# RWKV "wkv" recurrence on one core: rows of w and u on another queue, other tiles for the first loads, half of the last numerators in other PSUM banks, and a new hand-placed order at both ends

## The chip, the cores and the metric

The kernel runs on one core of one Trainium2 chip. The core has TensorE (PE; its weight loads are listed as PEld), VectorE (DVE), ScalarE (ACT), GpSimd (POOL) and SyncE (SP, used here only to issue DMAs). The metric is device time in microseconds (us) of one execution, as the median of several runs. All inputs lie in HBM and the output goes back there.

## The reference

For each of 16 batches and 256 channels a scalar recurrence runs over 2048 steps. It is cut here to one step:

```python
ww = u + kk                       # output of step t
qq = np.maximum(pp, ww)
e1 = np.exp(pp - qq); e2 = np.exp(ww - qq)
output[b, t, :] = (e1 * aa + e2 * vv) / (e1 * bb + e2 + 1e-08)
ww = pp - w + kk                  # state for step t + 1
qq = np.maximum(ww, kk)
e1 = np.exp(ww - qq); e2 = np.exp(kk - qq)
aa = e1 * aa + e2 * vv
bb = e1 * bb + e2
pp = qq
```

`k`, `v` and the output are (16, 2048, 256) in float32, 33.5 MB each; `w` and `u` have 256 values.

## The kernel before, in words

The 2048 steps are cut into 16 chunks `c` of 128 steps (two halves of 64), and the 16 batches into 4 groups of 4. One tile `n` (0 to 63) is one chunk of one group: `c, p = divmod(n, 4)`. It holds 128 steps on the partitions and 4 x 256 channels, 512 KB of `k` and as much of `v`. Inside a half, the recurrence is done with cumulative logarithms, triangular matrices and a division; between halves a small state is carried.

Each tile passes these steps, named as in the scheduler:

- `LK n`, `LV n`: the DMAs of k and v (lines 100 to 111). The first few go on SP (`n < BYSP`), the others on POOL's queue.
- `RK n`: k is rounded into a tile that PE may read (line 189, DVE or POOL, as `how(n)` says; "D" DVE, "P" POOL, "C" no rounding, the DMA writes such a tile itself).
- `R q n`, `L q n` (q = 0, 1): on PE, the rows of w and u (line 196), and then the cumulative sums of k (line 202), are added up in one of two PSUM tiles X, which are handed round in turn. (Each is a pair of PSUM banks; "a bank" means one X below.)
- `X q n`: ACT takes the exponential of X into a ring EZR of 11 tiles (line 205).
- `CV n`, `TV n`: v is cast to bf16 (line 209, DVE for n < 10, then POOL), and DVE multiplies it with both exponentials (line 214).
- `S n`: 8 matmuls of PE add up each half into TOT (line 240).
- `DEN n`, `NUM n`: 12 matmuls each on PE, the denominator into an X tile and the numerator into the one tile `num` (line 317), 10 tiles behind the exponentials.
- `LN n`, `INV n`: ACT forms ln of the denominator from X (line 325) and exp of its negative (line 329), in one of two tiles `rd`.
- `MUL n`: DVE multiplies numerator and inverse into an output tile `ot` (line 337).
- `ST n`: SP stores it in one DMA of 256 KB and two of 128 KB (lines 350 and 343). From tile 52 on the last 128 KB go on POOL's queue as `SQ n`.

Once in a chunk, when `S` of its four tiles is done, the state moves on: `CS` (DVE copies TOT), `TU` (PE turns it), `SL` (ACT), `FR`, `OF` (DVE), `SW` (ACT), `CH`, `SS`, `KP` (DVE), `TK` (PE turns it back), `BK` (DVE copies it for `DEN` and `NUM` of the next chunk) and `SN`.

Before some steps of PE the kernel issues matmuls of zeros into TURN, "zeros" (line 144): `Z` says how many before which step, `Z0` the same for tile and chunk 0. 38 stand at the very start.

The order of all this is written out by a small scheduler (lines 358 to 438). Each step has a place on an axis of tiles; the scheduler always emits the lowest place whose predecessors are done and whose buffer is free. The places come from the table `P`, by `n % 4` in the middle, with another slope for the last 10 tiles (`TAIL`). Every engine then executes its steps in the order of emission and waits by semaphores. Buffers are counted in `free`: `K` rounded k (4), `KP` raw k (5), `V` raw v (4), `VB` cast v (2), `N` the numerator's tile (1), `RD` (2), `OT` output tiles (8).

The rows of w and u go on ACT's DMA queue into one `rd` tile (line 117), and `wu` casts and combines them on DVE (lines 170 and 171).

Of the kernel before, what the change touches and what calls it, by code (L numbers as in the profile page):

```python
# [7 lines left out]
F32 = mybir.dt.float32  # L8
# [3 lines left out]
ACT = mybir.ActivationFunctionType  # L12
# [3 lines left out]
def kernel(  # L16
# [9 lines left out]
    K = tc.keep_in_program_order  # L26
# [10 lines left out]
    SOON = 0  # L37
    UNTIL = 16
# [10 lines left out]
    BYQ = "PSSP"  # L49
    BYF = 93  # L50
    FILL = 1
    P = {"LK": -4.45, "LV": -3.2, "RK": [-2.85, -1.165, -3.305, -1.485], "L": [-12.055, -8.285],
         "X": [-1.875, -0.74], "CV": [0.915, -1.225, -0.805, -4.96], "TV": [-1.505, 1.745, 1.29, 1.32],
         "S": [2.74, -4.135, 2.105, -1.96], "wu": -0.98, "mats": -9.17,
         "STATE": [[-7.49, 2.76, -5.41, 2.15, -0.24, 3.49, -6.31, -2.72, -4.26, 6.5, 5.66, 3.32], [2.48, -1.26, -10.66, 3.23, -8.74, -6.75, 4.23, 2.99, 4.44, -5.61, -28.95, -22.63], [-0.45, 0.53, 6.83, 8.8, 7.73, 14.16, 12.07, 7.09, 13.89, 18.61, 6.68, 11.48]],
         "R": [-0.795, -7.965],
         "OUT": {"DEN": [-0.47, -0.155, -0.55, -0.495], "LN": [-11.935, -9.86, -0.84, -6.17], "INV": [-13.87, -8.32, -4.99, -5.82], "NUM": [-0.105, 0.155, 0.11, -5.15], "MUL": [1.115, 0.345, 0.895, 1.035], "ST": [-5.05, 7.26, 1.245, 7.765], "SQ": [-3.365, 6.69, -2.4, 8.84]},
         "TAIL": {"DEN": -4.36, "LN": -16.54, "INV": 3.8, "NUM": -0.31, "MUL": 4.39, "ST": 14.35, "step": 2.989, "SQ": 26.08},
         "Z0": {"L": 1, "S": 3, "DEN": 0, "NUM": 6, "TK": 47, "TU": 17, "R": 12},
         "Z": {"DEN": 0, "L": 1, "NUM": 0, "TK": 4, "S": 0, "TU": 1, "R": 0}}  # L60

# [53 lines left out]

    def row_wu(x, g):
        K(SC.dma_start(out=WUf[g::32, :], in_=bass.AP(tensor=x.tensor, offset=x.offset, ap=[[0, 4], list(x.ap[0])])))
# [24 lines left out]
    def zeros(m, first=False):  # L142
        for j in range(m):
            K(PE.matmul(TURN[:, 0:192], Z[:, 0:128], Z, start=first, stop=True, skip_group_check=True))  # L144

    zeros(38, True)

# [175 lines left out]
    def log_den(n, a):  # L323
        rd = rpool.tile([128, 2, D], F32, tag="rd", name="rd")
        K(SC.activation(rd, X[a], ACT.Ln, scale=RS))  # L325
        RD[n] = rd

    def inverse(n):
        K(SC.activation(RD[n], RD[n], ACT.Exp, scale=-1.0))  # L329

    def num(n):
        NUM[n] = psn.tile([128, 2, D], F32, tag="num", name="num")
        apply(NUM[n], n, ("SN", "IdN"), 0)

    def mult(n):
        o = opool.tile([128, 4, Dm], F32, tag="ot", name="ot")
        K(DVE.tensor_mul(o.rearrange("p (i n) d -> p i (n d)", i=2), NUM.pop(n), RD.pop(n)))  # L337
        OT[n] = o
# [21 lines left out]
    def step(name, place, fn, args=(), after=(), take=None, give=(), mode=0):  # L360
        ops[name] = dict(place=place, fn=fn, args=args, after=list(after), take=take, give=give, mode=mode)

    for n in range(NP):
        c, j = divmod(n, 4)
        early = n < BYSP
        put = lambda key: n + P[key][j]
# [4 lines left out]
        kb = "V" if early else "KP" if how(n) != "C" else "K"  # L371
        if n:
            step(("LK", n), n + P["LK"], load_k, (n,), [("LK", n - 1)], kb)
        else:
            free["V"] -= 1
        step(("LV", n), n + P["LV"], load_v, (n,), [("LV", n - 1)] + ([("LK", n)] if n else []), "V")
        if how(n) != "C":
            step(("RK", n), put("RK"), round_k, (n,), [("LK", n), ("RK", n - 1)], "K", [kb])
        for q in range(2):
# [3 lines left out]
            step(("X", q, n), n + P["X"][q], exps, (n, q), [("L", q, n), ("NUM", n - RING), ("S", n - RING)], None, ["X"])  # L383
        step(("CV", n), put("CV"), cast_v, (n,), [("LV", n), ("CV", n - 1)], "VB", ["V"])
        step(("TV", n), put("TV"), times_v, (n,), [("X", 1, n), ("CV", n), ("TV", n - 1)], None, ["VB"])
# [13 lines left out]
        step(("INV", n), place("INV"), inverse, (n,), [("LN", n)])  # L399
        step(("NUM", n), place("NUM"), num, (n,), [("BK", c), ("TV", n), ("NUM", n - 1), "mats"], "N", mode=3)  # L400
        step(("MUL", n), place("MUL"), mult, (n,), [("NUM", n), ("INV", n), ("MUL", n - 1)], "OT", ["N", "RD"])
        step(("ST", n), place("ST"), store, (n,), [("MUL", n), ("ST", n - 1)], None, [] if shared(n) else ["OT"])
# [8 lines left out]
    while todo:  # L411
        for name in todo:
            o = ops[name]
            if all(x not in ops or "done" in ops[x] for x in o["after"]) and (xs if o["take"] == "X" else free.get(o["take"], 1)):
                break
        else:
            raise AssertionError(todo[:9])
        todo.remove(name)
        args = list(o["args"])
        if o["take"] == "X":  # L420
            held[name] = xs.pop(0)
            args.append(held[name])
# [4 lines left out]
        if o["give"] == ["X"]:  # L427
            x = held[("DEN", name[1]) if name[0] == "LN" else ("R",) + name[1:]]
            xs.append(x)
            args.append(x)  # L430
        else:
            for x in o["give"]:
                free[x] += 1
# [35 lines left out]
```

## Time and profile before

| what | value |
|---|---|
| median of 3 runs | 293.96 us (293.93 to 294.11) |
| profiled execution | 294.72 us, span of its instructions 293.0 us |
| granted TensorE clock, mean | 0.987 |
| DMA | 101.20 MB, mean 345 GB/s |
| ACT, line 205, 128 exponentials | 126.8 us busy, 1014 ns each |
| ACT, lines 329 and 325, 64 each | 67.8 and 65.7 us, 1059 and 1026 ns |
| DVE, lines 337 and 214, 64 each | 78.1 and 77.7 us, 1220 and 1217 ns |
| PE, zeros, line 144, 331 | 56.4 us busy |
| first exponential on ACT starts | 10.13 us |
| last product on DVE starts | 285.67 us |

The busy time of PE counts matmuls that overlap, so it is a share of time with a matmul under way and no measure of how much of the array is used. A line of a timeline gives the start, the time to the end of the last of its instructions, engine, line, operation, output and inputs, form and number; in brackets the idle time of the engine just before it and what ended that.

The program has three stages. In the fill, to about 48 us, loads, exponentials and the first state build up the distance of 10 tiles. In the middle, a tile takes 4.04 us. In the drain, from about 258 us, there are only outputs.

### The profile page before, as it was taken

The page shows a single profiled execution, that of the slowest core. Times are in us where ns is not written, and L with a number is a line of the kernel's source. Part 1 is how long each engine was busy: PE and PEld are TensorE (multiplying, and loading weights), DVE is VectorE, ACT ScalarE, POOL GpSimd, SP SyncE. Part 2 cuts the span into 40 slices and gives each one's busy share as a digit, 9 for nine tenths or more (in the row PEclk, how much of TensorE's full clock was granted, in tenths as well). Part 3 has the DMA queues.
Part 4 walks back from the last instruction along what each step waited for, and adds up shares of the span by engine and source line. Part 5 has one row for each costly group of instructions (what it writes and reads, how often), then busy time and mean ns, then how long its engine had stood idle before and what let it go on. Part 6 is the DMA issues. An engine that isn't in the chain of part 4 may idle for free.

```text
span 293.0 us, 8081 instructions
## 1 busy us (share of the span) xinstructions
PE 273.6 (93%) x3275; PEld 140.2 (48%) x3275; DVE 247.2 (84%) x422; ACT 258.7 (88%) x289; POOL 175.6 (60%) x218
## 2 busy tenths in 40 slices
PE   7899998999999999999999999999999999997750
PEld 7445743454545444444545444554544454543420
DVE  6574859989898989989898989899899989697751
ACT  1486498999999999999999999999999999997970
POOL 6167339575768677575767686775757574431230
PEclk9999999999999999999999999999999999999995
DMA  7999999999999999999999999999999999956884
GB/s 221 349 240 353 346 350 297 380 365 394 380 397 380 380 391 385 391 378 397 383 391 372 392 388 391 395 387 392 391 386 372 394 359 389 313 156 189 221 245 136
DMA packets 58549, 101.20 MB, mean 345 GB/s; under 512 B 5128, under 2 KB 43536, under 8 KB 58512
## 3 DMA queue, kind: packets, MB, share of 16 engines
q0 software_dynamic: 21216, 65.54, 64.8%
q1 hardware_dynamic: 37280, 35.14, 35.7%
q8 instruction: 25, 0.41, 0.6%
q14 instruction: 12, 0.10, 0.1%
q10 hardware_dynamic: 16, 0.01, 0.0%
HBM read 67.12 MB, written 33.55 MB: 344 GB/s over the span
## 4 chain that ended last, share of the span: by engine, by line
PE 70%; DMA 10%; DVE 5%; issue 5%; ACT 4%; POOL 3%; POOLq 0%; SPq 0%; ACTq 0%; DVEq 0%
PE X L202 17%; PE X L317 15%; PE num L317 12%; PE X L196 10%; PE TURN L144 9%; PE TOT L240 6%; DMA kf<-in_k_dram 4%; DMA vr<-in_v_dram 3%; DVE ot L337 2%; DMA WUf<-in_u_dram 2%; PE TOT L253 2%; ACT EZR L205 1%; DVE EZR L214 1%; PE TURN L297 1%; ACT rd L329 1%
## 5 line engine op out<-in xcount | busy, mean ns | idle before, releaser
L205 ACT ACTIVATE EZR<-X 128x1024 bf16<-128x1024 f32 x128 | 126.8, 1014 | 14.9 <-PE X L202 14.9
L209 POOL CAST vb<-vr 128x1024 bf16<-128x1024 f32 x54 | 56.4, 1044 | 71.3 <-DVE EZR L214 67.9
L337 DVE TENSOR_TENSOR ot<-num,rd 128x1024 f32<-128x1024 f32 x64 | 78.1, 1220 | 8.6 <-PE num L317 5.1
L214 DVE TENSOR_TENSOR EZR<-EZR,vb 128x2048 bf16<-128x2048 bf16 x64 | 77.7, 1217 | 0.3
L329 ACT ACTIVATE rd<-rd 128x1024 f32<-128x1024 f32 x64 | 67.8, 1059 | 2.0
L325 ACT ACTIVATE rd<-X 128x1024 f32<-128x1024 f32 x64 | 65.7, 1026 | 3.5 <-PE X L317 1.2
L144 PE MATMUL TURN<-Z 128*128 128x192 bf16 x331 | 56.4, 259 | 1.6 <-DVE Z L128 1.6
L110 POOL DMA_DIRECT2D vr<-in_v_dram x61 | 46.0, 755 | 13.9 <-DVE kr L189 7.1
L196 PE MATMUL X<-WU,CO 64*64 64x512 bf16 x512 | 51.9, 390 | 1.6 <-DVE WU L171 1.3
L144 PEld LDWEIGHTS <-Z 128*128 128x128 bf16 x331 | 29.6, 101 | 48.9 <-issue 47.1
L202 PE MATMUL X<-kr,NLE 128*128 128x512 f32 x128 | 45.6, 438 | 0.0
L202 PE MATMUL X<-kr,NLZ 128*128 128x512 f32 x128 | 45.5, 437 | 0.0
L103 POOL DMA_DIRECT2D kf<-in_k_dram x53 | 40.2, 758 | 0.0
L189 DVE CAST kr<-kf 128x1024 fp32r<-128x1024 f32 x39 | 32.0, 849 | 5.9 <-DMA kf<-in_k_dram 5.8
L317 PE MATMUL num<-EZR,SN 64*64 64x512 bf16 x256 | 25.9, 387 | 6.5 <-DVE ot L337 6.5
L196 PEld LDWEIGHTS <-CO 64*64 64x64 bf16 x512 | 15.7, 105 | 31.8 <-issue 26.9
L317 PE MATMUL X<-EZR,S 64*64 64x512 bf16 x256 | 26.2, 394 | 0.7 <-ACT EZR L205 0.3
L317 PE MATMUL X<-cb,Id 64*64 64x512 bf16 x256 | 25.8, 376 | 0.0
L317 PE MATMUL X<-EZR,Id 64*64 64x512 bf16 x256 | 25.8, 376 | 0.0
L317 PE MATMUL num<-cb,IdN 64*64 64x512 bf16 x256 | 25.8, 378 | 0.0
L317 PE MATMUL num<-EZR,IdN 64*64 64x512 bf16 x256 | 25.6, 376 | 0.0
L240 PE MATMUL TOT<-EZR,OH 128*32 128x256 bf16 x512 | 23.7, 277 | 1.2 <-DVE EZR L214 1.2
(63 smaller groups left out, 259.3 us busy)
## 6 DMA issues: line engine op xcount, KB each, us to landing
vr<-in_v_dram POOLq DMA_DIRECT2D x61, 512.0 KB, 7.8
kf<-in_k_dram POOLq DMA_DIRECT2D x53, 512.0 KB, 8.7
out_dram<-ot SPq DMA_DIRECT2D x64, 256.0 KB, 9.7
out_dram<-ot SPq DMA_DIRECT2D x116, 128.0 KB, 10.0
kr<-in_k_dram POOLq DMA_DIRECT2D x8, 512.0 KB, 8.5
vr<-in_k_dram SPq DMA_DIRECT2D x3, 512.0 KB, 5.2
vr<-in_v_dram SPq DMA_DIRECT2D x3, 512.0 KB, 6.1
out_dram<-ot POOLq DMA_DIRECT2D x12, 128.0 KB, 3.0
```

What stands on the lines that cost most here:

```text
L110: K((SP if n < BYSP else POOL).dma_start(out=vr, in_=rows_of(v, n)))
L144: K(PE.matmul(TURN[:, 0:192], Z[:, 0:128], Z, start=first, stop=True, skip_group_check=True))
L196: K(PE.matmul(X[a][o:o + HS, i, :].rearrange("p (n d) -> p n d", n=2), CO[r:r + HS, q, :], WU[r:r + HS, :].unsqueeze(1).broadcast_to([HS, ...
L202: K(PE.matmul(X[a][:, i, :], (NLE, NLZ)[q], km[:, i, :], start=False, stop=True, skip_group_check=True))
L205: K(SC.activation(ez(n)[:, q, 1], X[a], ACT.Exp))
L209: K((DVE if n < EARLY else POOL).tensor_copy(vb, VR.pop(n)))
L214: K(DVE.tensor_mul(ez(n)[:, :, 0], ez(n)[:, :, 1], vb.unsqueeze(1).broadcast_to([128, 2, 2, D])))
L240: K(PE.matmul(t[32 * j:32 * j + 32, 0:256], OH[:, s:s + 32], ez(n)[:, 0, 1 - q, i, 256 * x:256 * x + 256], start=p == 0 and x == 0, stop=p ...
L317: K(PE.matmul(out_tile[o:o + HS, i, :], left, right, start=s == 0, stop=s == 2, tile_position=(r, o), skip_group_check=True))
L325: K(SC.activation(rd, X[a], ACT.Ln, scale=RS))
L329: K(SC.activation(RD[n], RD[n], ACT.Exp, scale=-1.0))
L337: K(DVE.tensor_mul(o.rearrange("p (i n) d -> p i (n d)", i=2), NUM.pop(n), RD.pop(n)))
```

## The change

The diff has these parts.

1. The row of u and then that of w are loaded on SP's queue, right behind k 0, instead of w and u on ACT's. `wu` is placed ahead of the rounding of k 0.
2. `BYSP` 4 for 3: k 3 and v 3 also go on SP. The raw tiles of k 0 to k 3 and v 0 to v 2 are taken from the pool of output tiles, which now has 10 tiles (8 before). `NK` is 3 (4), `NV` 3 (4).
3. Which engine rounds the first 12 k is written out: `FIRST = "DPDCCCCCPCCP"`, with "D" for n < 4.
4. From tile 56 on, the numerators of odd tiles go to an X tile (`by_x`), which comes free when its product is done; the scheduler can therefore free two kinds of buffer in one step.
5. For the last tile, the inverse and the product are done in two halves.
6. The first zeros are 26 (38), those in the tables differ by a few; `TK` of the middle has 3 (4).
7. The table `P` has new values throughout, and a new table `AT` gives single steps a place of their own, for tiles 0 to 19 and 50 to 63; it overrides `P`.

```diff
-    BYSP = 3
+    BYSP = 4
-    NK, NKP, NV, NVB, NRD, NOT = 4, 5, 4, 2, 2, 8
+    NK, NKP, NV, NVB, NRD, NOT = 3, 5, 3, 2, 2, 10
-    CF = 11
+    FIRST = "DPDCCCCCPCCP"
+    VOT = 3
+    XT = 8
...
-         "S": [2.74, -4.135, 2.105, -1.96], "wu": -0.98, "mats": -9.17,
+         "S": [2.43, -4.915, 1.825, -2.27], "wu": -5.05, "mats": -9.3,
...
-         "Z0": {"L": 1, "S": 3, "DEN": 0, "NUM": 6, "TK": 47, "TU": 17, "R": 12},
-         "Z": {"DEN": 0, "L": 1, "NUM": 0, "TK": 4, "S": 0, "TU": 1, "R": 0}}
+         "Z0": {"L": 1, "S": 5, "DEN": 5, "NUM": 5, "TK": 50, "TU": 16, "R": 11},
+         "Z": {"DEN": 0, "L": 1, "NUM": 0, "TK": 3, "S": 0, "TU": 1, "R": 0}}
+    AT = {"LV 0": -4.6, "RK 0": -2.3975, "R 0 0": -1.8739, "L 0 0": -11.62, "X 0 0": -2.16, "R 1 0": -7.3021,
...
     def how(n):
-        return "D" if n < BYSP else "C" if n < CF else PLAN[n % len(PLAN)]
+        return "D" if n < BYSP else FIRST[n] if n < len(FIRST) else PLAN[n % len(PLAN)]
...
-            KR[n] = raw(vpool, "vr") if n < BYSP else raw(kppool, "kf")
+            KR[n] = raw(opool, "ot") if n < BYSP else raw(kppool, "kf")
...
-        vr = raw(vpool, "vr")
+        vr = raw(opool, "ot") if n < VOT else raw(vpool, "vr")
...
     load_k(0)
-    row_wu(w, 0)
-    row_wu(u, 1)
+    row_wu(SP, u, 1)
+    row_wu(SP, w, 0)
...
-    zeros(38, True)
+    zeros(26, True)
...
+    def parts(n):
+        return (slice(0, 1), slice(1, 2)) if n == NP - 1 else (slice(0, 2),)
+
     def inverse(n):
-        K(SC.activation(RD[n], RD[n], ACT.Exp, scale=-1.0))
+        for i in parts(n):
+            K(SC.activation(RD[n][:, i], RD[n][:, i], ACT.Exp, scale=-1.0))
+
+    def by_x(n):
+        return n >= NP - XT and n % 2 == 1
 
-    def num(n):
-        NUM[n] = psn.tile([128, 2, D], F32, tag="num", name="num")
+    def num(n, a=None):
+        NUM[n] = psn.tile([128, 2, D], F32, tag="num", name="num") if a is None else X[a]
         apply(NUM[n], n, ("SN", "IdN"), 0)
 
-    def mult(n):
+    def mult(n, a=None):
         o = opool.tile([128, 4, Dm], F32, tag="ot", name="ot")
-        K(DVE.tensor_mul(o.rearrange("p (i n) d -> p i (n d)", i=2), NUM.pop(n), RD.pop(n)))
+        for i in parts(n):
+            K(DVE.tensor_mul(o.rearrange("p (i n) d -> p i (n d)", i=2)[:, i], NUM[n][:, i], RD[n][:, i]))
         OT[n] = o
...
     def step(name, place, fn, args=(), after=(), take=None, give=(), mode=0):
-        ops[name] = dict(place=place, fn=fn, args=args, after=list(after), take=take, give=give, mode=mode)
+        key = name if isinstance(name, str) else " ".join(map(str, name))
+        ops[name] = dict(place=AT.get(key, place), fn=fn, args=args, after=list(after), take=take, give=give, mode=mode)
```

In the middle the new places (for `DEN` -0.375, -0.435, -0.235 and -0.715 by `n % 4`, before -0.47, -0.155, -0.55 and -0.495) put `S` of tiles 4c+1 and 4c+3 behind the `DEN` that they stood ahead of. On PE, one chunk then reads as follows (`D`, `N` for DEN and NUM, `R` for the rows and logs of both q, `z` for zeros before TK and TU):

```
before: D24 N24 R35 S32 S33 | D25 N25 R36 z4 TK7 | D26 S34 N26 R37 S35 | D27 N27 R38 z1 TU8
after:  D24 N24 R35 S32 | D25 S33 N25 R36 z3 TK7 | D26 S34 N26 R37 | D27 S35 N27 R38 z1 TU8
```

In the fill, `TU 0` comes ahead of the rows of tile 6 (before: tile 7), `S 4` goes ahead of the rows of tile 7 and `S 5` behind those of tile 8, and `S 9` comes behind `DEN 1`. In the drain, `S 60` to `S 63` stand together behind `NUM 54`.

More of the change, by code (lines that the diff above doesn't have):

```diff
@@ L374 @@
         else:
[L375 to L376 removed]
+            free["OT"] -= 1
+        step(("LV", n), n + P["LV"], load_v, (n,), [("LV", n - 1)] + ([("LK", n)] if n else []), vb)
         if how(n) != "C":
@@ L399 @@
         step(("INV", n), place("INV"), inverse, (n,), [("LN", n)])
-        step(("NUM", n), place("NUM"), num, (n,), [("BK", c), ("TV", n), ("NUM", n - 1), "mats"], "N", mode=3)
-        step(("MUL", n), place("MUL"), mult, (n,), [("NUM", n), ("INV", n), ("MUL", n - 1)], "OT", ["N", "RD"])
+        step(("NUM", n), place("NUM"), num, (n,), [("BK", c), ("TV", n), ("NUM", n - 1), "mats"], "X" if by_x(n) else "N", mode=3)
+        step(("MUL", n), place("MUL"), mult, (n,), [("NUM", n), ("INV", n), ("MUL", n - 1)], "OT", ["X" if by_x(n) else "N", "RD"])
         step(("ST", n), place("ST"), store, (n,), [("MUL", n), ("ST", n - 1)], None, [] if shared(n) else ["OT"])
@@ L426 @@
             args.append(held[("R",) + name[1:]])
[L427 to L433, printed above, removed]
+        for g in o["give"]:
+            if g == "X":
+                x = held[("DEN", name[1]) if name[0] == "LN" else ("NUM", name[1]) if name[0] == "MUL" else ("R",) + name[1:]]
+                xs.append(x)
+                args.append(x)
+            else:
+                free[g] += 1
         if o["mode"] and not quiet:
```

28 lines of the change are left out of this document (15 added, 13 removed), and 104 rows, old and new, of the table AT.

## The prediction

> **What bounds the kernel now.** I read the page first, then the table by stretches, then each engine's timeline in three places: the fill, one period of the steady middle, the drain.
>
> ```profile
> PE 273.6 (93%) x3275; PEld 140.2 (48%) x3275; DVE 247.2 (84%) x422; ACT 258.7 (88%) x289; POOL 175.6 (60%) x218
> GB/s 221 349 240 353 346 350 297 380 365 394 380 397 380 380 391 385 391 378 397 383 391 372 392 388 391 395 387 392 391 386 372 394 359 389 313 156 189 221 245 136
> PE 70%; DMA 10%; DVE 5%; issue 5%; ACT 4%; POOL 3%; POOLq 0%; SPq 0%; ACTq 0%; DVEq 0%
> ```
>
> The mean hides three stages. The table by stretches (busy us and instructions of PE, PEld, DVE, ACT, POOL; clock, DMA, GB/s) separates them.
>
> ```profile
> 10.10:31.60 21.50, 21.23 (x191) 11.67 (x190) 12.64 (x19) 16.89 (x18) 12.65 (x16) 1.00 1.27 312
> 140.00:180.00 40.00, 39.92 (x491) 20.03 (x491) 36.63 (x63) 39.44 (x46) 28.99 (x35) 1.00 1.05 386
> 258.00:284.50 26.50, 19.37 (x301) 10.11 (x295) 20.37 (x30) 23.98 (x27) 7.09 (x11) 1.00 0.69 198
> ```
>
> In the fill ACT is idle for 4.6 of 21.5 us. In the middle PE and ACT are both full: one chunk (four tiles) takes 16.18 us, from DEN 24 at 140.72 to DEN 28 at 156.90. In the drain ACT works 24.0 of 26.5 us. The middle on PE, DEN 25 to DEN 27 (L317 on X is DEN, on num NUM; L240 is S; L144 zeros; L297 TK):
>
> ```profile
> 144.06 0.66 PE L240 MATMUL TOT<-EZR,OH 128*32 128x256 bf16 x16
> 144.72 0.41 PE L317 MATMUL X<-EZR,S 64*64 64x512 bf16 x4
> ...
> 145.45 0.41 PE L317 MATMUL num<-EZR,SN 64*64 64x512 bf16 x4
> ...
> 148.05 0.51 PE L144 MATMUL TURN<-Z 128*128 128x192 bf16 x4
> 148.40 0.39 PE L297 MATMUL TURN<-Id,CB 128*128 128x128 bf16 x4
> 148.80 0.41 PE L317 MATMUL X<-EZR,S 64*64 64x512 bf16 x4
> ...
> 149.57 0.40 PE L240 MATMUL TOT<-EZR,OH 128*32 128x256 bf16 x8
> 149.91 0.41 PE L317 MATMUL num<-EZR,SN 64*64 64x512 bf16 x4
> ...
> 152.59 0.40 PE L240 MATMUL TOT<-EZR,OH 128*32 128x256 bf16 x8
> 152.93 0.41 PE L317 MATMUL X<-EZR,S 64*64 64x512 bf16 x4
> ```
>
> and the exponentials (L205) and the logarithm (L325) beside it on ACT:
>
> ```profile
> 147.75 1.92 ACT L205 ACTIVATE EZR<-X 128x1024 bf16<-128x1024 f32 x2
> 149.69 1.03 ACT L325 ACTIVATE rd<-X 128x1024 f32<-128x1024 f32 x1
> ```
>
> The reader is to see a loop. A DEN needs the bank that the exponential X 0 just before it frees. The first of the two at 147.75 ends at 148.75, DEN 26 starts at 148.80, its last matmul ends at 149.64 (0.84 after its start), LN 26 starts at 149.69. From one DEN to the next this loop takes 3.97 at least (0.89 DEN to LN, 3.03 LN to the end of X 0, 0.05). Four segments make a chunk: 4.00, 4.08, 4.13 and 3.97. Only the third is over the loop because of PE: X 0 37 frees its bank at 152.72, but S 35 stands ahead of DEN 27, which starts at 152.93. In the others PE arrives just in time. PE has no slack to give away, segment by segment.
>
> **The steady middle, part by part.** The scheduler's order of the changed kernel on PE, against that of before, shows three moves in most chunks.
> - S 35's kind goes from ahead of DEN 27 to behind it. Segment three falls to the loop's 3.97: -0.16. Segment four gets the S between DEN 27 and NUM 27. What that costs is in the third segment of before, where S 34 stands so: DEN to S 0.77, S to NUM 0.34, together 1.11, against 0.67 from DEN 27 (152.93) to NUM 27 (153.60). Segment four holds the turn TU too and is just full: 3.97 + 0.44 = 4.41.
> - S 33's kind goes from ahead of DEN 25, where it lay inside the wait for the bank, to behind it, into the segment with zeros and TK. That segment was 4.08, or 3.97 where its DEN did not wait (DEN 45 to 46). With 1.11 for 0.67 to 0.73, and one zero less (four take 148.05 to 148.40, 0.09 each), it becomes 4.345: +0.265.
> - Segment one loses an S but stays at the loop: -0.03.
>
> This order holds in 9 segments two, 12 segments four and 12 segments three between DEN 2 and DEN 53 (the placements keep the old order in a few chunks): 9 x 0.265 + 12 x 0.44 - 12 x 0.16 - 12 x 0.03 = +5.4. A one-off of 0.46 at DEN 45 (4.46 instead of 4.00), where a product on DVE came late, is covered by the slower pace, and three unchanged segments two lose a zero, -0.16. **Middle: +4.8.** Bounds: if PE only had to fit its work into the chunk, with no segment kept apart, 13.2 of tiles (four times 0.64 DEN, 0.65 NUM, 2.01 rows and logs), 1.75 of S (0.34 and three times 1.11 - 0.64), 0.665 of TK and zeros and 0.72 of TU are 16.33, +0.15 a chunk, +1.5 in ten chunks; and if an S behind DEN costs nothing, the saved 0.16s give -1.9. I take the segments, since DEN waits in PE's queue for X 0, and everything behind it waits too.
>
> The Trainium skill speaks of the same price: TensorEngine Tiling (Array Packing), Key Properties, says that a change of tiling mode drains the array. DEN and NUM use 64x64 tiles, S 128x32 ones; the rows agree (S to S 0.22 in the pair at 144.06, S to NUM 0.34, DEN to S 0.77 for 0.64). Without drains, 0.22 an S, the middle would be about +0.1 by the same count.
>
> The other edits there ride along. Three v buffers for four move every second v load behind a cast on POOL (LV 39 from 146.81 to about 153.1; CV 39 starts at 160.52, and loads issued there land after 7 to 10 us). The k and v landings come every 1.7 us without a hole, and fewer are queued ahead, so it should land near 158.4: 2 us of cover. Nothing is added. Raw tiles in outputs' tiles cost nothing either: the first product before was at 47.2, and these seven tiles are read within the first 20 us.
>
> **The fill.** The rows of w and u, issued on ACT at 1.23 and 2.36, land behind k 1 and v 0, and DVE waits for u until 8.14. On SP they follow k 0 directly, which lands 4.2 after its issue at 0.81, at 5.0. DVE is free at 5.52, casts the rows (0.29 + 0.48, 6.3) and then k 0 (0.69 to 1.00), now behind the rows. The logs start at 7.0 to 7.3 and ACT 0.75 later (9.38 to 10.13 before): 7.9 for 10.13, -2.2. The rounding and loading order behind it:
>
> ```profile
> 10.13 1.02 ACT L205 ACTIVATE EZR<-X 128x1024 bf16<-128x1024 f32 x1 [5.94 <-PE X L202]
> ...
> 35.98 2.02 ACT L205 ACTIVATE EZR<-X 128x1024 bf16<-128x1024 f32 x2 [4.37 <-PE X L202]
> ...
> 48.55 1.02 ACT L325 ACTIVATE rd<-X 128x1024 f32<-128x1024 f32 x1 [1.19 <-PE X L317]
> ```
>
> The 4.37 is X 0 8 behind TK 0 and its 47 zeros on PE (30.13 to 34.02). It stays: 50 zeros now. TU 0 with 16 zeros moves ahead of R 0 6 and costs ACT about 2.5 there (before 0.84 and 0.75 a tile later); S 4 and S 5 no longer stand ahead of R 0 8. X 0 8 comes out at 33.4, -2.5. The 1.19 was S 9, which waited on PE for its product ahead of DEN 1; it is now behind it, which saves 1.2 less the 0.4 of the 5 new zeros ahead of DEN 0: LN 1 at 45.4 for 48.55. The segment two that follows costs 0.3: DEN 2 at 48.9 for 51.79, -2.9. Against that, k 4 to k 7 now wait for one of three rounded buffers instead of four, and loads in this stretch land 7 to 8.7 after issue; I take **-2.6**, with ends -0.3 (all of the start lost again) and -3.2.
>
> **The drain.** Before, one bank holds the numerators: NUM waits for the product of the tile before, and a tile takes 2.22 (product 1.22, sequence 1.00).
>
> ```profile
> 282.37 0.41 PE L317 MATMUL num<-EZR,SN 64*64 64x512 bf16 x4 [0.73 <-DVE ot L337]
> ```
> ```profile
> 283.31 1.22 DVE L337 TENSOR_TENSOR ot<-num,rd 128x1024 f32<-128x1024 f32 x1 [1.00 <-PE num L317]
> 285.67 1.22 DVE L337 TENSOR_TENSOR ot<-num,rd 128x1024 f32<-128x1024 f32 x1 [1.14 <-PE num L317]
> ```
>
> With odd numerators in the banks of the logs ACT sets the pace: 1.065 to the inverse and 0.965 to the next logarithm, 2.03 to 2.08 a tile. I laid the new order on these durations from DEN 53. The state's stage (S 60 to S 63, now together behind NUM 54) still holds SL 15 until 7.6 after DEN 53 (7.8 before). The inverse of tile 62 ends 23.2 after it (before 282.30 - 258.35 = 23.95): -0.8. After that, before, NUM 63 waits for the product of 62 and the last product ends 4.6 later; now NUM 63 is there, and the last inverse and product go in halves: 1.03 + 0.53 + 0.65 + 0.6, 2.75 later. **-2.6 to the last product, -2.8 to the last landing** (the first half's store is already out). On POOL the quarter stores are reordered; SQ 62 and SQ 60 (0.6 each) fit between product 62 and the last half, so SQ 63 is not late. Bounds -2.0 and -3.2; the cover for the banks is that a numerator holds one for about 2 us of each 4.
>
> **Sum:** -2.6 + 4.8 - 2.8 = -0.6. The profiled execution took 294.72 (span 293.0); the median of the runs is 293.96, 0.76 less. So 294.1 for a profiled one, **293.4** by the median: fill and drain pay for a slower middle.
>
> **Rivals.**
> - *The S behind DEN is hidden* (0.20). If PE overlaps the small sums with the numerators, the middle stays or loses the 0.16s: -5.4 to -7.3, 288.6 to 286.7. For it: PE is called busy all the time, with modelled ends. Against: the starts 148.80, 149.57, 149.91 are plain.
> - *Slower: the loads in the fill cannot keep up with three rounded-k buffers* (0.22). k 6 may be issued only when the logs of k 3 end, about 16.4, and is needed at 23.8; k 7 about 18.9 and 26.2. So a landing of more than 7.4 us after issue delays ACT by the rest. Loads 5 to 10 took 6.9 to 11.0 before; at 10 the 2.6 are gone: 293.96 + 4.8 - 2.8 = 296.0. For it: these latencies. Against: they are queueing, and fewer loads are queued now.
> - *The rows come no earlier* (0.08): if u lands behind v 0 again, the start's 2.2 are lost: 295.6.
>
> **How the numbers follow.** The forecast has 0.50, with a range of its own of 291.9 to 294.9 from the ends of the terms. Of it 0.25 lies over 0.2% (0.59 us) below the median, about what a measurement of this kernel can tell, 0.17 within, 0.08 above. With the first rival faster has 0.45; the two slow ones, mostly above the bound, give slower 0.35 and same 0.20. The range for 8 in 10 takes in most of both sides: 288.2 to 296.2.
>
> **What would show it.** Right: ACT's first exponential near 7.9; LN 1 near 45.4 for 48.55; chunks of 16.7 in the middle with segments near 4.0, 4.35, 4.0, 4.4 and S 0.77 behind DEN; ACT idle there; a drain of 2.05 a tile and no wait of NUM for a product. Wrong: chunks of 16.2 or less; an exponential in the fill that waits for a k load; the first exponential at 9 or later; a v cast on POOL that waits for its load.

## The result, and the profile after

The changed kernel takes 296.87 us (median), beside 293.94 us for the kernel before in the same comparison: a ratio of 1.010, 95% interval 1.0066 to 1.0133. It is slower by about 2.9 us, where 0.6 faster was forecast. Its profiled execution took 297.04 us with a span of 295.3 (before 294.72 and 293.0). Of all the runs below, two of the seventh experiment's ten were in a slower state of the chip, by 1 to 2%, and are left out of its numbers.

The page's first part, its GB/s row (40 slices of 7.4 us) and the sum of the chain of waits, after:

```profile
PE 273.4 (93%) x3254; PEld 133.8 (45%) x3254; DVE 246.2 (83%) x424; ACT 260.5 (88%) x290; POOL 173.5 (59%) x217
...
GB/s 174 351 351 344 323 343 301 376 368 388 367 382 385 383 359 386 379 354 393 350 392 381 389 380 386 383 363 382 379 387 381 385 381 371 364 155 137 226 269 159
...
PE 41%; ACT 23%; DMA 19%; DVE 6%; issue 4%; POOL 2%; SPq 2%; POOLq 0%; DVEq 0%
```

The busy times hardly differ, so this part can't tell what happened. The chain can: ahead of it stood PE with 70%, now PE has 41, and DMA and ACT have taken the rest. The chain is no longer held by one engine. Where the time went is read from the starts of DEN on PE, which cut the span at the same work in both kernels:

| stretch | before | after | difference | forecast |
|---|---|---|---|---|
| start to DEN 2 | 51.72 | 50.03 | -1.69 | -2.6 |
| DEN 2 to DEN 53 | 206.63 | 212.54 | +5.91 | +4.8 |
| DEN 53 to the end | 34.65 | 32.73 | -1.92 | -2.8 |
| span | 293.0 | 295.3 | +2.3 | -0.6 |

All three signs are right, and in this pair of profiles all three sizes are off by about 1 us in the same direction. That turned the sum. The first row is the least certain. DEN 2 comes between 49.83 and 50.88 in the eight profiles that have the changed kernel's order up to there (mean 50.3), and at 51.72, 50.78 and 50.90 in the three with the order of before (mean 51.1). By these means the fill gained 0.8 rather than 1.69, and the three rows add up to +3.2, beside +2.9 by the medians.

**The steady middle.** The timeline of PE after, DEN 25 to DEN 28 (L426 is DEN on X and NUM on num, L349 S, L253 zeros, L406 TK, L362 TU):

```profile
146.95 0.41 PE L426 MATMUL X<-EZR,S 64*64 64x512 bf16 x4 [0.23 <-ACT EZR L314]
...
147.72 0.40 PE L349 MATMUL TOT<-EZR,OH 128*32 128x256 bf16 x8
148.05 0.41 PE L426 MATMUL num<-EZR,SN 64*64 64x512 bf16 x4
...
150.91 0.39 PE L406 MATMUL TURN<-Id,CB 128*128 128x128 bf16 x4
151.23 0.41 PE L426 MATMUL X<-EZR,S 64*64 64x512 bf16 x4
...
155.20 0.41 PE L426 MATMUL X<-EZR,S 64*64 64x512 bf16 x4
...
155.97 0.40 PE L349 MATMUL TOT<-EZR,OH 128*32 128x256 bf16 x8
156.30 0.41 PE L426 MATMUL num<-EZR,SN 64*64 64x512 bf16 x4
...
159.00 0.61 PE L362 MATMUL TOT<-Sel,ts 128*128 128x96 f32 x4
159.54 0.41 PE L426 MATMUL X<-EZR,S 64*64 64x512 bf16 x4
```

The S (147.72, 155.97) stands 0.77 behind its DEN, and NUM 0.33 behind that. The segments are 4.28 (146.95 to 151.23), 3.97, 4.34, and 3.97 for the one before: 16.57 a chunk, for 16.18. In the two long ones DEN starts 0.25 and 0.43 after X 0 has freed its bank: PE is late.

**Three long segments.** Between DEN 4 and DEN 21 three segments are far longer: 5.02 (DEN 5), 4.47 (DEN 13), 4.65 (DEN 21). At the second, PE waits for a product on DVE:

```profile
93.55 0.41 PE L426 MATMUL num<-EZR,SN 64*64 64x512 bf16 x4 [0.61 <-DVE ot L454]
```

DVE after, at that place, the rounding RK 24 (L298) and the product MUL 11 (L454):

```profile
90.70 1.66 DVE L298 CAST kr<-kf 128x1024 fp32r<-128x1024 f32 x1 [0.86 <-DMA kf<-in_k_dram]
92.29 1.21 DVE L454 TENSOR_TENSOR ot<-num,rd 128x1024 f32<-128x1024 f32 x1
```

POOL after, its casts RK 23 (L298) and CV 22 (L318):

```profile
89.78 1.05 POOL L298 CAST kr<-kf 128x1024 fp32r<-128x1024 f32 x1
90.76 1.05 POOL L318 CAST vb<-vr 128x1024 bf16<-128x1024 f32 x1
```

A rounding on DVE lasts 0.68 in most places, here 1.66, and it ends 0.55 after POOL's second cast (91.81). It also starts late, since k 24 came 0.86 after DVE was free for it. The product is queued behind it, NUM 12 behind the product, the rows and logs of the next tiles behind NUM 12.

**Fill.** ACT after, its first exponential (X 0 0), X 0 3, X 0 4 and X 0 8:

```profile
7.57 1.02 ACT L314 ACTIVATE EZR<-X 128x1024 bf16<-128x1024 f32 x1 [5.49 <-PE X L311]
...
16.17 2.05 ACT L314 ACTIVATE EZR<-X 128x1024 bf16<-128x1024 f32 x2 [0.87 <-PE X L311]
...
19.23 2.04 ACT L314 ACTIVATE EZR<-X 128x1024 bf16<-128x1024 f32 x2 [1.00 <-PE X L311]
...
34.83 2.02 ACT L314 ACTIVATE EZR<-X 128x1024 bf16<-128x1024 f32 x2 [4.07 <-PE X L311]
```

The start is 2.56 earlier than before. At X 0 4 (before 20.61) 1.38 of it is left, at X 0 8 (before 35.98) 1.15; LN 1 comes at 46.64 for 48.55.

The 7.57 itself is in part luck. On PE, 37 zeros (the first 26 and the 11 of `R`) stand ahead of the first rows:

```profile
1.65 4.87 PE L253 MATMUL TURN<-Z 128*128 128x192 bf16 x37 [1.65 <-DVE Z L237]
6.45 0.41 PE L305 MATMUL X<-WU,CO 64*64 64x512 bf16 x4
```

These zeros start every 0.16 us until the trace's clock record reaches full speed, and every 0.083 us from there on. Here that is at 5.1 us. In five other profiles with the same order (first, third, eighth, ninth and eleventh experiment) it is at 6.7 to 7.3 us, and the first exponential comes at 8.35 to 8.66.

**Drain.** Products on DVE after, and the last stores of SP and POOL (each line an issue):

```profile
281.44 1.23 DVE L454 TENSOR_TENSOR ot<-num,rd 128x1024 f32<-128x1024 f32 x1 [0.77 <-DMA out_dram<-ot]
283.44 1.23 DVE L454 TENSOR_TENSOR ot<-X,rd 128x1024 f32<-128x1024 f32 x1 [0.77 <-ACT rd L442]
285.44 1.23 DVE L454 TENSOR_TENSOR ot<-num,rd 128x1024 f32<-128x1024 f32 x1 [0.77 <-DMA out_dram<-ot]
287.02 1.29 DVE L454 TENSOR_TENSOR ot<-X,rd 128x512 f32<-128x512 f32 x2 [0.35 <-DMA out_dram<-ot]
```
```profile
286.70 0.38 SPq L467 DMA_DIRECT2D out_dram<-ot  x1
287.12 0.60 SPq L460 DMA_DIRECT2D out_dram<-ot  x1
287.82 0.55 SPq L467 DMA_DIRECT2D out_dram<-ot  x1
288.46 0.61 SPq L460 DMA_DIRECT2D out_dram<-ot  x1
```
```profile
286.97 1.20 POOL L460 DMA_DIRECT2D out_dram<-ot  x2 [1.40 <-DVE ot L454]
288.60 0.60 POOL L460 DMA_DIRECT2D out_dram<-ot  x1 [0.44 <-DVE ot L454]
```

A tile takes 2.00, and ACT sets this pace: the inverse of tile 62 ends at 285.41, 0.03 before its product starts, although the bracket there names a DMA. The last product ends at 288.31, 25.74 after DEN 53 (before 28.54). But from there to the end it is 6.99 now, 6.12 before. The last store lands 5.02 after the last product (before 3.46), and the end comes 2.01 after that (before 2.65). The stores of tiles 62 and 63 are issued within 2 us, and at 286.97 POOL issues two in a row: SQ 62 and, behind it, SQ 60, whose product had ended at 282.67.

### The profile page after: what moved, and what is told of

Its sections match the earlier page's. It is cut to its first block, busy times and chain, and to the rows that moved or that the text cites. A ratio compares the mean times of both kernels' runs of the same rounds, so it can differ in the third digit from the quotient of the medians.

```text
span 295.3 us, 8061 instructions
## 1 busy us (share of the span) xinstructions
PE 273.4 (93%) x3254; PEld 133.8 (45%) x3254; DVE 246.2 (83%) x424; ACT 260.5 (88%) x290; POOL 173.5 (59%) x217
## 4 chain that ended last, share of the span: by engine, by line
PE 41%; ACT 23%; DMA 19%; DVE 6%; issue 4%; POOL 2%; SPq 2%; POOLq 0%; DVEq 0%
PE X L426 12%; DMA kf<-in_k_dram 8%; PE X L311 8%; ACT rd L434 8%; ACT rd L442 8%; ACT EZR L314 7%; DMA out_dram<-ot 7%; PE num L426 7%; PE X L305 4%; PE TURN L253 4%; DVE ot L454 4%; DMA ot<-in_v_dram 3%; PE TOT L349 3%; PE TOT L362 2%; PE TURN L406 1%
## 5 line engine op out<-in xcount | busy, mean ns | idle before, releaser
L314 ACT ACTIVATE EZR<-X 128x1024 bf16<-128x1024 f32 x128 | 128.2, 1015 | 16.7 <-PE X L311 16.6
L318 POOL CAST vb<-vr 128x1024 bf16<-128x1024 f32 x54 | 57.3, 1061 | 66.5 <-DVE EZR L323 56.8
L454 DVE TENSOR_TENSOR ot<-num,rd 128x1024 f32<-128x1024 f32 x60 | 73.1, 1218 | 10.2 <-ACT rd L442 8.5
L442 ACT ACTIVATE rd<-rd 128x1024 f32<-128x1024 f32 (+1 forms) x65 | 67.9, 1045 | 2.0
L253 PE MATMUL TURN<-Z 128*128 128x192 bf16 x310 | 54.7, 260 | 1.6 <-DVE Z L237 1.6
L253 PEld LDWEIGHTS <-Z 128*128 128x128 bf16 x310 | 27.8, 101 | 48.3 <-issue 46.5
L212 POOL DMA_DIRECT2D kf<-in_k_dram x54 | 42.3, 787 | 1.1 <-issue 1.1
L298 DVE CAST kr<-kf 128x1024 fp32r<-128x1024 f32 x39 | 29.5, 784 | 3.7 <-DMA kf<-in_k_dram 3.7
L426 PE MATMUL X<-EZR,S 64*64 64x512 bf16 x256 | 26.2, 396 | 6.1 <-ACT rd L434 2.5
L426 PE MATMUL num<-EZR,SN 64*64 64x512 bf16 x240 | 24.3, 391 | 3.4 <-DVE ot L454 3.4
L426 PE MATMUL X<-cb,Id 64*64 64x512 bf16 x256 | 25.5, 376 | 0.0
L426 PE MATMUL X<-EZR,Id 64*64 64x512 bf16 x256 | 25.5, 376 | 0.0
L349 PE MATMUL TOT<-EZR,OH 128*32 128x256 bf16 x512 | 24.3, 277 | 0.0
L426 PE MATMUL num<-cb,IdN 64*64 64x512 bf16 x240 | 23.6, 376 | 0.0
L426 PE MATMUL num<-EZR,IdN 64*64 64x512 bf16 x240 | 23.6, 376 | 0.0
```

The source lines that it names most:

```text
L314: K(SC.activation(ez(n)[:, q, 1], X[a], ACT.Exp))
L318: K((DVE if n < EARLY else POOL).tensor_copy(vb, VR.pop(n)))
L426: K(PE.matmul(out_tile[o:o + HS, i, :], left, right, start=s == 0, stop=s == 2, tile_position=(r, o), skip_group_check=True))
L442: K(SC.activation(RD[n][:, i], RD[n][:, i], ACT.Exp, scale=-1.0))
L454: K(DVE.tensor_mul(o.rearrange("p (i n) d -> p i (n d)", i=2)[:, i], NUM[n][:, i], RD[n][:, i]))
```

## The experiments

The numbers are those of the labels; there is no fifth. "Ratio" is to the kernel before, run on the same chip in the same comparison, with its 95% interval; the changed kernel stands at 1.0100. DEN 2, middle (DEN 2 to DEN 53), drain (DEN 53 to the end of the span) and the segments of the middle over 4.4 us, named by the DEN that ends them, are from the profiled execution alone.

| run | median | ratio | DEN 2 | middle | drain | segments over 4.4 |
|---|---|---|---|---|---|---|
| before | 293.94 | | 51.72 | 206.63 | 34.65 | DEN 45 |
| after | 296.87 | 1.0100 (1.0066 to 1.0133) | 50.03 | 212.54 | 32.73 | 5, 13, 21 |
| e1_s_ahead | 293.73 | 0.9986 (0.9955 to 1.0016) | 50.29 | 209.51 | 32.30 | 5, 13, 21 |
| e2_s_behind | 298.39 | 1.0138 (1.0092 to 1.0184) | 50.78 | 211.66 | 34.46 | |
| e3_less_stored | 297.39 | 1.0114 (1.0083 to 1.0144) | 50.30 | 211.49 | 32.91 | 13, 21 |
| e4_before_less_stored | 293.20 | 0.9979 (0.9958 to 1.0001) | 50.90 | 206.22 | 34.38 | |
| e6_rk_behind | 292.78 | 0.9951 (0.9925 to 0.9977) | 50.88 | 207.93 | 32.29 | 43, 46 |
| e7_rows_alone | 293.56 | 0.9972 (0.9943 to 1.0001) | 50.12 | 206.95 | 35.03 | 29, 41 |
| e8_one_bank | 295.73 | 1.0056 (1.0027 to 1.0085) | 50.63 | 207.83 | 37.34 | |
| e9_sq_order | 291.83 | 0.9917 (0.9886 to 0.9947) | 50.07 | 207.41 | 31.92 | 49 |
| e10_k1_act | 291.88 | 0.9924 (0.9899 to 0.9948) | 50.28 | 207.08 | 32.24 | |
| e11_last_act | 291.42 | 0.9911 (0.9881 to 0.9942) | 50.51 | 207.56 | 30.53 | |
| e12_both | 290.42 | 0.9883 (0.9857 to 0.9909) | 50.29 | 207.24 | 30.67 | |
| e13_four_k | 291.99 | 0.9939 (0.9913 to 0.9964) | 50.68 | 208.47 | 30.85 | 29, 46 |
| e14_four_v | 291.78 | 0.9934 (0.9910 to 0.9959) | 50.72 | 208.62 | 30.66 | 29, 45 |
| e15_rk_only | 295.36 | 1.0065 (1.0041 to 1.0089) | 49.83 | 210.40 | 33.07 | |

**First: S ahead of DEN again** (changed kernel).

```diff
+    for n in range(5, 50):
+        if n % 4 in (1, 3) and n != 9:
+            ops[("DEN", n)]["place"] = max(ops[("DEN", n)]["place"], ops[("TV", n + 8)]["place"] + 0.005)
```

> The changed kernel with one thing undone: on PE the S of every second tile (S 13, S 15, ... S 55) goes back ahead of the DEN that it fell behind, in tiles 5 to 49; nothing moves on another engine. Theory PE order (an S between DEN and NUM sets the pace, 16.57 us a chunk instead of 16.18): chunks of 16.18 from DEN 5 on, 11 x 0.39 = -4.3, about 292.6 us. Rival, loads (the DMAs work without a pause at 375 to 390 GB/s in both kernels, and k 16, 24 and 32 land 0.09 us before their rounding starts): up to DEN 23 nothing can come sooner, then 30 tiles at 16.18 a chunk at best, -2.9 or less, 294.0 to 296.9, and new waits for k in the tiles after 24. If the S is free: 296.9, no change.

The time falls by 3.1, almost all that the change had cost. Chunks away from the three long segments are 16.18. PE of this run, S 32 and S 33 in one go ahead of DEN 25, and NUM 25 0.74 behind DEN:

```profile
145.40 0.66 PE L349 MATMUL TOT<-EZR,OH 128*32 128x256 bf16 x16
146.06 0.41 PE L426 MATMUL X<-EZR,S 64*64 64x512 bf16 x4
...
146.80 0.41 PE L426 MATMUL num<-EZR,SN 64*64 64x512 bf16 x4
```

The three long segments stay, and get longer (5.51, 4.68, 4.68). So the median lies nearer to the rival's 294.0 than to 292.6, and the run alone does not tell whether the DMAs limit it; the third and fourth do.

**Second: S behind DEN in the kernel before.**

```diff
+    for n in range(5, 50):
+        if n % 4 in (1, 3):
+            ops[("DEN", n)]["place"] = min(ops[("DEN", n)]["place"], ops[("TV", n + 8)]["place"] - 0.002)
```

> The kernel before with only this moved on PE: in tiles 5 to 49 the S of every second tile goes behind DEN, as in the changed kernel; nothing moves on another engine. Theory PE order: 12 chunks of 16.57 for 16.18, +4.3 (less what waits for k give back, such as the 0.46 at DEN 45), 297.8 to 298.3 us. Rival, loads: the middle before already goes at the pace of the DMAs (389 GB/s), but a slower PE adds to it all the same: it gives the same sign, +2 to +4. If the S is free: 293.9.

4.1 slower by the ratio and 4.7 by the medians (298.39 for 293.68 in its comparison), with chunks of 16.64 to 16.66 for 16.18. No other engine's order moves in this run or in the first, so the price of S behind DEN is shown from both sides. The long segment at DEN 45 is gone.

**Third and fourth: fewer bytes.** Both kernels store only the first half of each output up to tile 47.

```diff
-    for h in range(1 if shared(n) else 2):
+    for h in range(0 if n < 48 else 1 if shared(n) else 2):
```

> The changed kernel with less DMA work: of tiles 0 to 47 only the first 256 KB of the 512 KB of output are stored (the second half of these outputs is left out), 12.6 of 101 MB; the order of the engines is the same. Theory PE order: steady chunks stay 16.57; only the three one-off waits for k 16, k 24 and k 32 go, -2.2, about 294.7 us. Rival, loads: chunks fall under 16.4 and the time to 292 or less.

> The kernel before with the same left out (the second 256 KB of the outputs of tiles 0 to 47). Theory PE order: the chunk of 16.18 is the loop of PE and ACT and stays; only the one-off wait at DEN 45 goes, 293.4 us. Rival, loads: the 16.18 are 6.3 MB at 389 GB/s, so with 5.2 MB a chunk they fall towards the loop's 15.9 to 16.0 and the time by 2 or more, under 292.

The kernel before keeps its chunk of 16.18 within 0.01. The table by stretches of the fourth run (columns as in the prediction):

```profile
140.00:172.00 32.00, 31.96 (x394) 15.69 (x389) 30.06 (x49) 31.50 (x36) 22.46 (x26) 1.00 0.97 329
```

329 GB/s for 385 in the same stretch of the kernel before, at the same pace: the loop of PE and ACT sets it, not the DMAs, although they show a share of about 1.0 in both. The rival "loads" falls as a bound of the chunk. In the third run one long segment goes (DEN 5), two stay, and the time does not fall, which my expectation did not have. DVE of the third run at the second place, and POOL beside it:

```profile
89.23 2.37 DVE L298 CAST kr<-kf 128x1024 fp32r<-128x1024 f32 x1 [0.16 <-DMA kf<-in_k_dram]
91.52 1.21 DVE L454 TENSOR_TENSOR ot<-num,rd 128x1024 f32<-128x1024 f32 x1
```
```profile
89.01 1.05 POOL L298 CAST kr<-kf 128x1024 fp32r<-128x1024 f32 x1
89.99 1.05 POOL L318 CAST vb<-vr 128x1024 bf16<-128x1024 f32 x1
```

Here k 24 is late by 0.16 only, and the rounding takes 2.37 instead. Both of POOL's casts take their usual 1.05; DVE's gets through when the second ends at 91.04, and needs 0.55 more. So at the second and third place (RK 32 starts with no wait for its k and lasts 2.60) the stall is the rounding beside two casts of POOL, and not the late k. At the first the late k has a part: in the changed kernel RK 16 waits 1.01 for k 16, falls beside CV 14 and ends at 59.14; here k 16 is there in time, the rounding ends at 57.65, and the long segment goes.

**Sixth: the three roundings behind the product** (first experiment's kernel).

```diff
+    for n in (16, 24, 32):
+        ops[("RK", n)]["place"] = ops[("MUL", n - 13)]["place"] + 0.005
```

> The changed kernel with the S ahead again (as in the first experiment), and on DVE the rounding RK 16, RK 24 and RK 32 one step later, behind the product MUL 3, 11 and 19, as in the later chunks; nothing moves on PE, ACT or POOL. Theory casts: the three long segments (DEN 5 at 5.5, DEN 13 and DEN 21 at 4.7 instead of 4.0 to 4.1) come from a rounding on DVE that lasts 1.6 to 2.4 us instead of 0.68 while POOL casts, with a product queued behind it; with the product ahead they go: -2.7, about 291.0 us. Rival, late loads (the rounding starts 0.09 us after k lands): the logs of k 16, 24, 32 come later still, and ACT waits for them: no gain, 293.7.

DVE of this run at the same place:

```profile
90.62 1.23 DVE L454 TENSOR_TENSOR ot<-num,rd 128x1024 f32<-128x1024 f32 x1 [1.34 <-ACT rd L442]
91.76 0.70 DVE L298 CAST kr<-kf 128x1024 fp32r<-128x1024 f32 x1
```

The rounding falls behind POOL's casts and lasts 0.70 (RK 24 and RK 32; RK 16 0.95). The three long segments are gone, and no exponential waits for these k. But by the ratios only 1.0 of the 2.7 arrives: two new long segments come near the end of the middle (4.68 at DEN 43, 4.60 at DEN 46). Shortly before each, a cast on POOL waits for its v (3.80 and 1.73 us); that this makes them is not shown.

**Fifteenth: the roundings alone.** The same edit on the changed kernel, S left behind DEN.

> The changed kernel with only the three roundings RK 16, 24 and 32 moved behind MUL 3, 11 and 19 on DVE; the S stay behind DEN. Theory casts: the three long segments (5.02, 4.47 and 4.65) become 3.97, -2.2, and nothing gives it back, because chunks of 16.57 leave the loads time: 294.7 us. Rival, loads: the segments after 32 get longer instead, 296 or more.

The middle falls by 2.14, as expected, and no segment is over 4.4; the time falls by 1.5 by the medians and 1.0 by the ratios, less than the 2.2 expected. So the three roundings cost 2.1 of the 5.9 in the middle. The rest, 3.8, fits S behind DEN, for which the first experiment gave 3.0 while its long segments grew by 0.7.

**Seventh: the rows alone on SP** (kernel before).

```diff
-    row_wu(w, 0)
-    row_wu(u, 1)
+    row_wu(SP, u, 1)
+    row_wu(SP, w, 0)
...
-         "wu": -0.98
+         "wu": -5.05
```

> The kernel before with only the rows of u and w moved to SP behind k 0, and cast on DVE ahead of RK 0. Theory walk (what the first exponential gains reaches LN 1): first exponential at about 7.6 for 10.1 and DEN 2 1.7 or more earlier, 292.2 us or less. Rival, loads set the fill: u, w and k 0 leave a hole in the DMAs of about 1.2 us at 4 to 5.5, so the loads from v 0 on land later than before; the first exponential comes earlier, but from X 0 2 on ACT waits for loads and nothing is left at DEN 2: 293.9 to 295.

The first exponential is at 9.63 only. PE of this run:

```profile
1.65 6.93 PE L144 MATMUL TURN<-Z 128*128 128x192 bf16 x50 [1.65 <-DVE Z L128]
8.51 0.41 PE L196 MATMUL X<-WU,CO 64*64 64x512 bf16 x4
```

The rows are cast by 6.64, but 50 zeros (38 and 12) stand ahead of them, and full clock comes at 7.1 us. Even in the profile before, with full clock at 5.3 us, the 50 zeros end only at 7.68. So the early start of the changed kernel needs its 26 zeros for 38 as well as the queue of the rows.

Still DEN 2 comes at 50.12, 1.6 earlier than in the profile before and 0.7 to 0.8 earlier than in the second and fourth run, about as in the changed kernel with 7.57. Little of that is the start walking through: X 0 8 comes at 35.56 (35.70 to 35.98 in those three), and most of the gain arises between DEN 0 and DEN 1 (4.61 for 5.04 to 5.71). So Walk has the size at DEN 2 and not the way there, and its 292.2 is missed. The sum is -0.8 by the ratio, with an interval that reaches no change: the middle has two long segments for one, and the drain is 0.4 longer.

**Eighth: one tile for all numerators** (sixth's kernel, `XT = 0`).

> The sixth experiment's kernel (S ahead, three roundings later) with all numerators in the one tile num (XT = 0); the halves of the last tile stay. Theory: in the drain each numerator waits for the product before it, 2.22 a tile instead of 2.0 from about tile 58 on: 6 x 0.2 = +1.2 to +1.7 on the kernel with XT = 8. If the numerators' banks do nothing: no difference.

+3.0 in the median and +5.05 in the drain, more than expected. Products are 2.2 to 3.4 apart: the hand-placed order (DEN 62 and 63 together ahead of NUM 62, for instance) needs the second place for numerators. A part may be the clock: it falls to a mean of 0.71 and 0.72 between 274 and 282 us, where PE waits for products (1.00 in the sixth run), and the four matmuls of a group then take 0.64 to 0.70 for 0.41. So this run shows what the new order is worth with its banks, not what the banks alone are worth.

**Ninth: quarter stores in order** (sixth's kernel).

```diff
+    at = 0
+    for n in range(54, 63):
+        at = max(at, ops[("ST", n)]["place"]) + 0.005
+        ops[("SQ", n)]["place"] = at
```

> The sixth experiment's kernel with the quarter stores on POOL's queue in the order of their tiles (before: 54, 56, 57, 55, 59, 58, 61, 62, 60, 63). Theory tail: the store of tile 60 is issued about 4.5 us earlier, so 128 KB fewer stand before the stores of tile 63 in the last 5 us: -0.3 to -0.6 against the sixth. If the end does not hang on the queue: the same.

By the ratios -1.0. The profiled spans differ by 1.7: 0.8 up to DEN 2, which scatters by as much, 0.5 in the middle (one long segment, at DEN 49, for those at DEN 43 and 46), and 0.37 in the drain. The tenth run keeps this order of the stores and has a drain of 32.24, so even the 0.37 is not shown to come from the order.

**Tenth, eleventh, twelfth** (on the ninth's kernel): k 1 issued on ACT's queue behind k 0; the last two quarter stores on ACT's queue; both.

```diff
+    KR[1] = raw(opool, "ot")
+    K(SC.dma_start(out=KR[1], in_=rows_of(k, 1)))
...
-        piece(n, 1, POOL)
+        piece(n, 1, SC if n >= 62 else POOL)
```

> The ninth experiment's kernel with k 1 issued on ACT's queue at the start, so that its data fill the hole of the DMAs while SP issues the rows of u and w. Theory loads (in the fill of the changed kernel X 0 4 waits for k 4, which lands at 18.4 because 1.2 us of DMA time were lost at 4 to 5.5): k 4 lands about 1.2 earlier, DEN 2 at 49.3 or less for 50.07, and -0.5 to -0.8 in the end: 291.1 to 291.4 us. Rival, walk of the state (X 0 8 behind TK 0 and its zeros sets LN 1, whatever the loads do): DEN 2 and the time unchanged.

> The ninth experiment's kernel with the quarter stores of tiles 62 and 63 issued on ACT's queue, where nothing is left to do, instead of POOL's. Theory issue (the end waits for the queue that issues the last quarter): -0.3 to -0.5. Rival, bytes (the last 900 KB after product 62 take what they take): no difference, within 0.2.

> Both edits together. If they are independent, the sum of the two differences; by the theories loads and issue 290.6 to 291.1 us, by their rivals 291.8.

In the tenth k 4 lands at 17.24 (18.41 in the changed kernel), as expected, and nothing follows from it: X 0 4 comes at 19.48, DEN 2 at 50.28. The rival's numbers hold. The run showed another wait in the fill. DVE of the tenth run, RK 3:

```profile
15.17 0.69 DVE L302 CAST kr<-ot 128x1024 fp32r<-128x1024 f32 x1 [1.53 <-PE X L315]
```

k 3 had landed at 11.24. RK 3 waits for the logs of k 2, since k 4 and k 5 were given the first two of the three rounded tiles to come free. The eleventh shortens the drain by 1.4, the median by 0.4. Only 0.2 of the 1.4 lies between the last product and the last landing (3.93 for 4.14); the rest lies behind the landing, from which the end is 0.90 away for 2.06. POOL closes with an instruction, DRAIN, that ends 1.5 us after the last store on its queue has landed: in the ninth at 288.65 (landed 287.12), the last thing to be waited for; in the eleventh at 285.17 (landed 283.72), before the other stores land at 287.74. The theory issue holds by this wait.

The twelfth is faster than the ninth by 1.4, where the tenth gave nothing and the eleventh 0.4; the intervals are too wide to tell more than a sum. It is the fastest: 290.42 us, a ratio of 0.9883 (0.9857 to 0.9909) to the kernel before, 3.4 us faster than it, with no long segment.

**Thirteenth and fourteenth** (on the twelfth's kernel): `NK` 4 and `NOT` 9, RK 3 earlier; `NV` 4 and `NOT` 9.

> The kernel of the run with both edits (k 1 on ACT's queue, last quarters on ACT's queue), with four tiles for rounded k (one output tile fewer), RK 3 on DVE ahead of CV 0, and RK 40 kept behind MUL 27 (behind SN 8). Theory buffer (in the fill of the changed kernel k 4 and k 5 are given two of the three rounded tiles ahead of RK 3, so RK 3 waits for the logs of k 2, and X 0 3 with it): X 0 3 about 0.7 earlier after X 0 0 (7.9 to 7.2 from start to start), DEN 2 at 49.6 for 50.3, about -0.6 in the end, 289.8 us. Rival, walk: X 0 4 to X 0 8 take up what X 0 3 gains, DEN 2 stays at 50.3 and the time at 290.4.

> The kernel of the run with both edits (290.42 us) with four tiles for raw v and nine for outputs, and RK 40 kept behind MUL 27 (behind SN 8). Theory v buffers (with three, every second v load is issued late, behind a cast on POOL, and the casts there wait for v): no wait of a cast on POOL for v above 0.5 in the middle, no segment over 4.4, runs closer together, 289.9 to 290.4. Rival, DMA pace (388 GB/s leave nothing to fetch earlier): waits and time as before, 290.4 to 291.

In the thirteenth X 0 3 comes at 16.18 for 16.69 and X 0 8 at 34.76 for 35.10, and by X 0 10 the gain is gone (40.09 for 39.98); DEN 2 is at 50.68. In the fourteenth casts on POOL still wait up to 2.6 for v, and long segments come at DEN 29 and 45. Both are slower than the twelfth, by 1.4 to 1.6. Neither buffer was what was short; both runs have nine output tiles, and whether that makes the late segments was not tried.

## Why the prediction was wrong

**The middle.** The mechanism was right: S behind DEN, segments with PE late, and a loop that passes it on. The term "9 x 0.265 + 12 x 0.44" was too large: measured 0.20 (4.28 for 4.08) and 0.37 (4.34 for 3.97), because DEN follows TK by 0.32 and TU by 0.54 when it does not wait, and I had used the rows where it does (0.40 and 0.62). That makes 0.39 a chunk, and about 3.0 to 3.8 in all (the first experiment, and the 5.91 less the roundings' 2.1), for 5.4, or 4.8 with the two small terms behind it.

The step that failed is the next one: "a one-off of 0.46 at DEN 45 ... is covered by the slower pace". It was covered, but three others came, 2.1 us by the fifteenth run, a term that the prediction put at nothing. So the 4.8 lies nearer to 5.91 than its parts do: a term too large by about 1 stood against a missing one of 2.1. The signs of the missing one were in the profile before. DVE there, RK 56 and MUL 43, and POOL's cast beside them:

```profile
220.17 1.51 DVE L189 CAST kr<-kf 128x1024 fp32r<-128x1024 f32 x1 [0.79 <-DMA kf<-in_k_dram]
221.61 1.21 DVE L337 TENSOR_TENSOR ot<-num,rd 128x1024 f32<-128x1024 f32 x1
```
```profile
220.09 1.05 POOL L189 CAST kr<-kf 128x1024 fp32r<-128x1024 f32 x1
```

The rounding lasts 1.51 instead of 0.68, and the product waits behind it; the rounding of every fourth tile of that profile, RK 16, RK 20 and so on to RK 60, lasts 0.77 to 1.51 beside a cast of POOL. I had read the late product as a one-off and not asked why. In the changed kernel the hand-placed places of MUL 3, 11 and 19 put RK 16, 24 and 32 ahead of these products and beside POOL's casts; at RK 20, 28, 36 and all from RK 40 on the order is the other way round, and there is no stall.

"Three v buffers ... nothing is added": the reasoning was wrong, since LV 39 landed at 162.60 and not near 158.4, and casts on POOL waited 9.4 us for v in five waits (before 3.4 in one), a sign of being wrong that the prediction had named. In the changed kernel no segment got long by it, and a fourth v tile (with one output tile fewer) gained nothing; whether these waits make the late segments of the sixth run stays open.

**The fill.** The start was near (7.57 for 7.9), with the luck of an early full clock. The step that failed is that the start's gain would last ("X 0 8 comes out at 33.4"; it was 34.83; of the 2.6 forecast for DEN 2, 0.8 is left by the means above). 0.7 goes at X 0 3, where RK 3 stands on DVE behind CV 1, which waits for v 1 until 14.03; without that it would still have waited for the logs of k 2, to 14.24. At X 0 4 an exponential does wait for a k load, another sign of being wrong that was named: k 4 lands at 18.41, 8.6 after its issue, and the logs start at 18.46. The tenth, thirteenth and seventh runs say more: with the first exponential at 7.57, 8.80, 8.81 or 9.63, DEN 2 stays between 50.0 and 50.7, no more than it scatters with the order unchanged. What sets it in that range isn't settled. The end of -0.3 that I had given for k 4 to k 7 did not come: k 6 and k 7 landed 6.1 and 6.0 after issue. (DEN 2 before stands at 51.72 in the trace, not 51.79.)

**The drain.** 2.00 a tile for 2.03 to 2.08, the inverse of tile 62 22.84 after DEN 53 for 23.2, the last product 2.80 earlier for 2.6. What failed is the step from there to the last landing, which is only 1.25 earlier for 2.8 (30.76 after DEN 53, before 32.01). "The first half's store is already out" is wrong: it is issued at 287.82, 0.49 before the last product ends, and lands 4.85 later. "SQ 63 is not late" holds for the issue (POOL is idle for 0.44 before it), but it lands 4.43 after it, where the last stores before took 2.9 to 3.0. With tiles closer together the stores of 62 and 63 are under way at once, with SQ 60 among them; that this makes the landings long is likely and not shown apart. 1.56 is lost from product to landing, and 0.64 comes back between landing and end; why is open. The 1.4 of the eleventh run is mostly POOL's closing wait, which the kernel before has too.

**The rivals.** "Slower: the loads in the fill" had the sign and nearly the time (296.0), but not the mechanism: it spoke of k 6 and k 7, whose landings beyond 7.4 us did not occur (k 4's 8.6 did, and the tenth run shows that it cost nothing at DEN 2), and the missing term lies in the middle. "The S behind DEN is hidden" is excluded by the first two runs, "the rows come no earlier" by the start.

## What to carry to other kernels

When an instruction in a profile lasts twice as long in some places as in others, find what runs beside it there before costing a change that moves it: its price depends on its neighbours on another engine. Cut two traces at the same work (here at DEN 2 and DEN 53) and compare stretch by stretch; three small misses of one sign were worth more than the forecast. Several profiles of one order say how far a stretch can be read: here DEN 2 scattered by 1 us. A gain at the very start of a pipeline is only what is left of it at the first place where something else is waited for.

## What was not expected of the hardware

In these traces roundings on DVE and casts on POOL exclude each other. A rounding on DVE of 0.68 lasted 1.66 and 2.37 beside casts of POOL, which kept their 1.05, and each time it ended 0.55 after POOL's last. In the profile before it also went the other way: RK 28 on DVE waited for one cast of POOL, went next, and POOL's RK 27 lasted 1.50:

```profile
106.00 1.40 DVE L189 CAST kr<-kf 128x1024 fp32r<-128x1024 f32 x1
```
```profile
106.80 1.50 POOL L189 CAST kr<-kf 128x1024 fp32r<-128x1024 f32 x1
```

The Trainium skill, SBUF — State Buffer, section "Who interferes with whom", says that DVE and GpSimd share a pair of ports as an exclusive lock and that the order of issue decides who is blocked. These rows agree on the exclusion, and on the order only in part: in the third run POOL's second cast (89.99) went ahead of a rounding that had stood since 89.23. Why it did there and not at RK 28 is open.

DMA engines with a share of about 1.0 were not the bound: with a sixth of each chunk's bytes gone, the share was 0.97 for 1.04, the rate 329 GB/s for 385, and the chunk stayed at 16.18.

The moment at which TensorE gets its full clock differed between profiles of the same order at the start, from 5.1 to 7.3 us, and with it the pace of the zeros (0.16 us each, then 0.083) and the first exponential (7.57 to 8.66).

The kernels here whose last quarter store goes on POOL's queue ended 2.0 to 2.7 us after their last landing, the eleventh to fourteenth, with it on ACT's queue, 0.9 after it.
